# A hybrid attention and DeltaNet layer on one core: the inverse's solved blocks are loaded into the inverse's own buffer, and the delays of the work streams are set anew

## The chip, the core and the metric

One NeuronCore of a Trainium2 chip runs the whole layer as one program. It has a matrix engine (TensorE, PE in the rows, with its weight loads as PEld), a vector engine (VectorE, DVE), a scalar engine (ScalarE, ACT), GpSimd (POOL) and a queue engine (SyncE, SP) that issues DMA transfers; POOL issues some too. Every engine takes its own list of instructions strictly in order, and they wait for one another through semaphores. The metric is the device time of one execution in microseconds (us). Before the change the median of three runs was 639.21 us (635.7 to 640.05).

## The reference, cut to what matters

One sequence of 512 tokens, model width 1024, fp32. One input projection feeds eight heads of block-sparse attention and eight heads of gated DeltaNet; their outputs are joined, projected, normed and added to x, and a squared-ReLU MLP with 4096 hidden columns follows.

```python
h = rms_norm(x, pre_mix_norm[l])
proj = jnp.einsum('bsd,dc->bsc', h, w_in[l])
...
o_att = moba_attention(q, k, v, rel_bias)       # 8 heads of 64, blocks of 256 keys
...
# gated DeltaNet, chunks of 64 tokens, per head and chunk:
m = jnp.where(strict, jnp.einsum('bhnid,bhnjd->bhnij', k_beta, kc) * decay, 0.0)
a_mat = m + jnp.eye(C, dtype=jnp.float32)
uw = lax.linalg.triangular_solve(a_mat, rhs, left_side=True, lower=True, unit_diagonal=True)
u, w = uw[..., :dh], uw[..., dh:]
def step(state, xs):                             # over the 8 chunks
    v_new = u_c - jnp.einsum('bhck,bhkv->bhcv', w_c, state)
    o = jnp.einsum('bhck,bhkv->bhcv', q_c, state) + jnp.einsum('bhcs,bhsv->bhcv', a_c, v_new)
    state = state * gl[..., None, None] + jnp.einsum('bhck,bhcv->bhkv', k_c, v_new)
...
x = x + rms_norm(mix, post_mix_norm[l])
m = jnp.square(jax.nn.relu(rms_norm(x, ...) @ w_up)) @ w_down
x = x + rms_norm(m, post_mlp_norm[l])
```

## The kernel before

**Matmuls.** Each fp32 product is made of three matmuls of split operands (`mm3`: high by high, high by low, low by high). So every weight chunk is loaded to `w_raw` (two buffers), cast to `w_hi` on ACT (line 205), and its low part `w_lo` is taken by a subtraction on DVE or POOL (line 206). The string `LO` says for each chunk which of the two: 'v' for DVE, 'p' for POOL. Results stand in PSUM banks named ps_mm, ps_g and ps_a.

**Order of the work.** The kernel is written as some thirty generators ("streams"): `projections`, `chunks` (the DeltaNet operands), `inverse`, `scan`, `scores` and `values` (attention), `weights_out`, `output` and others. A small class `Weave` runs them against a virtual clock, `weave.now`, that advances by the columns of each matmul. A stream yields a delay (from the tables `WAIT` and `DELAY`) or the name of a mark that another stream sets, and is resumed when the clock has come that far; among those that are due the lower `RANK` goes first. PE's order is the order in which this loop emits matmuls, and is fixed by hand. DVE, ACT, POOL and, for most of the program, SP get their order from a scheduler with priorities (`LEAD`, `PRIO`). `ORDER` and `START` say in which order the projection's column groups come and when streams are started.

**The solve.** The triangular solve of each 64 by 64 chunk is done by halves of 32. `inverse()` inverts all diagonal 32 by 32 blocks at once on DVE, 31 steps of a product (line 880) and a subtraction (line 881) with partitions as blocks, makes the transposed blocks (line 884), and stores both to two DRAM tensors, `d_u` (line 885) and `d_t` (line 886). `scan()` loads them back in the layout that PE wants: `UT` (128 x 2048, a buffer of the shared tag `big`, which has 14 of them, zeroed by POOL on line 892) takes four loads of `d_u` (line 900), and two small tiles `uap` take four loads of `d_t` (line 897). Then three groups of matmuls follow: `p1` (128 of 32 by 32, `NT` by `uap`), copied back into `uap` by ACT (line 913); `p2` (128 of 32 by 32, `uap` by `UT`), whose negative goes into the missing corner of `UT` (line 926); and the products of `UT` with `kB` and `vB`. With these the scan over the chunks begins, in which the state `S` goes from PE to DVE (lines 999, 1000) and back.

**After the mix.** Each of four row tiles of 128 tokens is normed (lines 1124 to 1135: statistics on ACT, a power on POOL at line 243, the product `xs` on DVE at line 1135), then turned by eight transposes on PE, and feeds the MLP. POOL adds split operands for the MLP on line 1347.

Of the kernel before, what the change touches and what calls it, by code (L numbers as in the profile page):

```python
# [19 lines left out]
WAIT = {'h': 0.26, 'conv_k': 5.48, 'k': 6.88, 'conv_q': 8.11, 'q': 1.52, 'conv_v': 12.72, 'v': 2.29, 'z': 11.49, 'ab': 0.67, 'g': 9.16, 'scalars': 55.01, 'r_in': 0.0, 'r_out': 30.56, 'kk': 3.56, 'kk_out': 93.91, 'gl': 0.0, 'qk': 13.83, 'va': 1.36, 'a': 6.03, 'row': 1.56, 'rows': 4.29, 'pv': 2.34, 'att': 1.98, 'inverse': 0.76, 'merge': 6.6, 'p1': 2.26, 'p2': 223.99, 'w': 1.15, 'vn': 1.06, 'state': 0.64, 'o_in': 5.67, 'o': 1.23, 'wo': 1.48, 'wo_out': 0.86, 'normed3': 7.36, 'normed': 18.07, 'n': 2.53, 'up': 2.92, 'sums': 0.12, 'turned': 11.21, 'pv0': 3.36, 'wv': 3.58}  # L20

RANK = {'chunks': 5, 'inverse': 3, 'scan': 2, 'scores': 5, 'values': 4, 'finish_o': 2, 'take': 1}
LEAD = {'chunks': 30, 'inverse': 100, 'scan': 100, 'scores': 0, 'values': 0, 'finish_o': 100, 'take': 300, 'take_a': 100}
# [1612 lines left out]
```

## Time and profile before

| | before |
|---|---|
| median of three runs | 639.21 us (639.21, 635.7, 640.05) |
| the profiled execution's own time | 639.11 us |
| its span, first to last instruction | 637.3 us |
| mean granted TensorE clock | 0.993 of 2.4 GHz |
| busy share PE, DVE, ACT, POOL | 97%, 76%, 58%, 21% |

The span is 1.8 us shorter than the execution's own time, and that execution lies 0.1 us below the median. In a row of the timeline the first number is the start, the second the duration of the group (or the time from the first start to the last end), and in brackets at the end stands how long the engine was idle before and which instruction ended that. A matmul's duration includes its way through the array; matmuls in a row start 0.23 us apart at 512 columns, so starts, not durations, tell PE's pace. "PEclk" is the granted clock as a share of 2.4 GHz: 0.50 is 1.2 GHz.

### The profile page before, as it was taken

To read this page: it belongs to the slowest core of one execution; us is meant where nothing else is said; L and a number is where in the kernel's file an instruction comes from. 1 tells how busy PE (TensorE), PEld (TensorE's weight loads), DVE (VectorE), ACT (ScalarE), POOL (GpSimd) and SP (SyncE) were. 2 spreads that over 40 slices of the span, in tenths; PEclk is the share of its full clock that TensorE was granted. 3 is DMA by queue.
4 is the path that set the end of the run, shared out by engine and by line. 5 is a ranking of instruction groups with operands and counts; after the bars stand their busy time and mean duration, and the time that the engine had idled before them with its cause. 6 is when DMAs were issued, how large, how long until landed. Compare 5 with 4: busy or idle time off the path is not lost.

```text
span 637.3 us, 11091 instructions
## 1 busy us (share of the span) xinstructions
PE 620.8 (97%) x4291; PEld 535.8 (84%) x4291; DVE 484.4 (76%) x725; ACT 370.3 (58%) x620; POOL 136.1 (21%) x173
## 2 busy tenths in 40 slices
...
PEclk9999999999979999999999999999999999999999
...
GB/s 223 131 76 65 101 100 143 107 102 146 113 120 37 41 61 138 247 96 166 117 361 248 175 296 241 255 262 233 280 257 340 298 291 285 261 212 298 180 0 133
DMA packets 61270, 115.26 MB, mean 181 GB/s; under 512 B 15862, under 2 KB 35449, under 8 KB 60834
## 3 DMA queue, kind: packets, MB, share of 16 engines
...
q10 hardware_dynamic: 294, 0.27, 0.1%
q14 instruction: 18, 0.15, 0.1%
...
## 4 chain that ended last, share of the span: by engine, by line
PE 81%; DVE 6%; DMA 5%; ACT 3%; POOL 1%; issue 1%; SPq 1%; POOLq 0%; DVEq 0%; ACTq 0%
PE ps_mm L148 40%; PE ps_g L148 22%; PE ps_a L148 16%; DMA wo_raw<-in_w_out 1%; PE ps_a L152 1%; DMA xx<-in_x 1%; PE ps_g L152 1%; DVE conv L488 1%; DMA wd<-d_T 1%; DVE S L999 1%; DMA nb<-in_pre_mix 1%; DMA uap<-d_t 1%; DVE S L1000 1%; POOL oss L243 1%; SPq L900 1%
## 5 line engine op out<-in xcount | busy, mean ns | idle before, releaser
L181 ACT CAST wdh<-wd 128x1024 fp32r<-128x1024 f32 x53 | 55.6, 1050 | 51.2 <-PE ps_mm L148 23.6
L182 DVE TENSOR_TENSOR u_l<-w,u_h 128x1024 fp32r<-128x1024 f32 x46 | 56.2, 1224 | 37.9 <-ACT u_h L181 37.9
L182 DVE TENSOR_TENSOR wdl<-wd,wdh 128x1024 fp32r<-128x1024 f32 x53 | 64.9, 1225 | 22.8 <-ACT wdh L181 22.7
L181 ACT CAST u_h<-w 128x1024 fp32r<-128x1024 f32 x46 | 47.8, 1044 | 57.2 <-PE ps_a L148 19.8
L148 PE MATMUL ps_mm<-hT_h,w_hi 128*128 128x512 f32 (+1 forms) x192 | 76.4, 403 | 0.2 <-ACT hT_h L314 0.2
L148 PE MATMUL ps_mm<-hT_h,w_lo 128*128 128x512 f32 (+1 forms) x192 | 72.9, 385 | 0.0
L148 PE MATMUL ps_mm<-hT_l,w_hi 128*128 128x512 f32 (+1 forms) x192 | 72.6, 383 | 0.0
L1306 POOL DMA_DIRECT2D d_T<-in_w_down x32 | 33.1, 1034 | 143.6 <-DMA d_T<-in_w_down 82.3
L205 ACT CAST w_hi<-w_raw 128x512 fp32r<-128x512 f32 x56 | 34.8, 622 | 37.0 <-PE ps_mm L148 15.9
L206 POOL TENSOR_TENSOR w_lo<-w_raw,w_hi 128x512 fp32r<-128x512 f32 x21 | 27.2, 1294 | 97.2 <-ACT w_hi L205 94.2
L148 PE MATMUL ps_mm<-wdh,u_h 128*128 128x512 f32 x116 | 45.2, 390 | 0.0
L148 PE MATMUL ps_mm<-wdl,u_h 128*128 128x512 f32 x116 | 45.1, 389 | 0.0
L148 PE MATMUL ps_mm<-wdh,u_l 128*128 128x512 f32 x116 | 45.1, 389 | 0.0
L148 PEld LDWEIGHTS ps_mm<-hT_h,w_lo 128*128 128x128 f32 x192 | 35.8, 189 | 7.5
L148 PEld LDWEIGHTS ps_mm<-hT_h,w_hi 128*128 128x128 f32 x192 | 36.0, 190 | 6.6 <-issue 0.5
L148 PEld LDWEIGHTS ps_mm<-hT_l,w_hi 128*128 128x128 f32 x192 | 36.1, 190 | 5.4
L182 DVE TENSOR_TENSOR u_l<-f,u_h 128x1024 fp32r<-128x1024 f32 x28 | 34.1, 1218 | 0.0
L148 PE MATMUL ps_g<-wdh,u_h 128*128 128x512 f32 x80 | 31.2, 390 | 0.4 <-DVE y L1480 0.4
L148 PE MATMUL ps_g<-wdh,u_l 128*128 128x512 f32 x80 | 31.1, 389 | 0.0
L148 PE MATMUL ps_g<-wdl,u_h 128*128 128x512 f32 x80 | 31.1, 389 | 0.0
L206 DVE TENSOR_TENSOR w_lo<-w_raw,w_hi 128x512 fp32r<-128x512 f32 x35 | 24.4, 696 | 8.2 <-ACT w_hi L205 7.1
L488 DVE SCALAR_TENSOR_TENSOR conv<-ps_mm,cw,conv 128x511 f32<-128x511 f32 (+2 forms) x36 | 26.8, 746 | 4.1 <-ACT conv L485 3.4
(461 smaller groups left out, 1867.4 us busy)
## 6 DMA issues: line engine op xcount, KB each, us to landing
d_T<-in_w_down POOLq DMA_DIRECT2D x48, 512.0 KB, 10.8
wd<-d_T SPq DMA_DIRECT2D x32, 512.0 KB, 6.2
w<-in_w_up SPq DMA_DIRECT2D x28, 512.0 KB, 7.7
wd<-in_w_down SPq DMA_DIRECT2D x24, 512.0 KB, 6.7
w_raw<-in_w_in SPq DMA_DIRECT2D x46, 256.0 KB, 2.7
wo_raw<-in_w_out SPq DMA_DIRECT2D x16, 256.0 KB, 2.9
d_T<-d_T POOLq DMA_DIRECT2D x8, 512.0 KB, 11.0
xx<-in_x SPq DMA_DIRECT2D x4, 512.0 KB, 7.4
```

What stands on the lines that cost most here:

```text
L148: nc.tensor.matmul(o, l, r, **kw)
L152: nc.tensor.transpose(o, i, ident[:k, :k])
L181: nc.scalar.copy(hi, src)
L182: tt(lo, src, f32(hi), op=OP.subtract)
L205: nc.scalar.copy(hi, raw)
L206: (sub or tt)(lo, raw, f32(hi), op=OP.subtract)
L243: nc.gpsimd.tensor_tensor(r, r, m, op=OP.pow)
L488: stt(c[:, s:], p[:, :512 - s], cw[:, ft, j:j + 1], c[:, s:], op0=OP.mult, op1=OP.add)
L900: nc.sync.dma_start(z3(UT[32 * b:32 * b + 32, :, :, o:o + 32]), d_u[b].rearrange("z j i -> j z i"))
L999: tt(Sn[hs, :, hs], S[hs, :, hs], EGL[hs, :, n:n + 1].to_broadcast([64, 4, 64]), op=OP.mult)
L1000: tt(Sn[hs, :, hs], Sn[hs, :, hs], sp[n][cs, hh::2], op=OP.add)
L1306: nc.gpsimd.dma_start(d_T[t][k], block(b, second)[k], accum_op=OP.add, max_dma_last_dim=1024)
```

## The change

The solved blocks, which `inverse()` holds in one tile `inv` of 128 x 2048, are viewed there as `UT`. Right behind the two stores, six loads bring the blocks back in PE's layout into that same tile, and two POOL memsets of 32 x 32 x 32 clear the corners. `scan()` no longer has a `UT` buffer of its own, its memset or its eight loads; `p1` reads the transposed blocks from the corner of `UT` that `p2`'s result overwrites later. The tables are new: of `WAIT` 36 entries differ, of `DELAY` 123, of `PRIO` 38; five weight chunks more have their low part on DVE.

```diff
-RANK = {'chunks': 5, 'inverse': 3, 'scan': 2, 'scores': 5, 'values': 4, 'finish_o': 2, 'take': 1}
+RANK = {'chunks': 1, 'inverse': 1, 'scan': 1, 'scores': 5, 'values': 4, 'finish_o': 3, 'take': 1}
...
-LO = 'ppvvpvpvpppvvvvppvvvvvvvvvvvvvvvpvvppvvvppppvppvppvvvpvvvvvvvvvv'
+LO = 'ppvvpvpvvppvvvvpvvvpvvvvvvvvvvvvvvvvppvvvvvpvppvppvvvpvvpvvvvvvv'
...
     def inverse():
...
         nc.sync.dma_start(d_t.rearrange("b z j i -> (b z) (j i)"), iT.rearrange("p j i -> p (j i)"))
+        UT = inv.rearrange("p a j i -> p (a j i)").rearrange("p (h t e) -> p h t e", h=8, t=4)
+        merged.append(UT)
+        for c in range(2):
+            nc.sync.dma_start(z3(UT[left[c], :, :, second]), d_t[2 * c].rearrange("z j i -> j z i"))
+        for c in range(2):
+            nc.sync.dma_start(z3(UT[right[c], :, :, second]), d_u[2 * c + 1].rearrange("z j i -> j z i"))
+        for c in range(2):
+            nc.sync.dma_start(z3(UT[left[c], :, :, first]), d_u[2 * c].rearrange("z j i -> j z i"))
+            nc.gpsimd.memset(UT[right[c], :, :, first], 0.0)
         mark("inverse")
...
     def scan():
-        UT = big("UT", (128, 8, 4, 64))
-        nc.gpsimd.memset(UT, 0.0)
-        uap = [sc.tile([128, 4, 4, 32], FT, name="uap", tag="ot", bufs=4) for _ in range(2)]
-        z3 = lambda a: a.rearrange("p h t i -> p (h t) i")
-        for c in range(2):
-            for z in range(2):
-                nc.sync.dma_start(z3(uap[z][64 * c:64 * c + 32]), d_t[2 * c, 16 * z:16 * z + 16].rearrange("z j i -> j z i"))
-        for b in range(4):
-            o = 32 * (b % 2)
-            nc.sync.dma_start(z3(UT[32 * b:32 * b + 32, :, :, o:o + 32]), d_u[b].rearrange("z j i -> j z i"))
+        UT = merged[0]
+        half = [sc.tile([128, 4, 4, 32], FT, name="half", tag="ot", bufs=4) for _ in range(2)]
         yield WAIT["merge"]
...
-                        mm(p1[b, h, t], NT[a, 4 * z + h, t, 32:64], uap[z][a, h, t], start=True, stop=True,
+                        mm(p1[right[c], h, t], NT[left[c], 4 * z + h, t, second], UT[left[c], 4 * z + h, t, second], start=True, stop=True,
...
-                        mm(p2[a, h, t], uap[z][b, h, t], UT[b, 4 * z + h, t, 32:64], start=True, stop=True,
+                        mm(p2[left[c], h, t], half[z][right[c], h, t], UT[right[c], 4 * z + h, t, second], start=True, stop=True,
```

What moves, as the instruction lists of the two programs have it (line numbers of the change are two to six higher). First SP around the stores and the loads of the solved blocks; `w_raw` are weight chunks of the projection, `E`, `pt` and `wo_raw` belong to attention and the out projection. Before:

```order
L885 DMA d_u<-inv 128x1024
L200 DMA w_raw<-in_w_in 128x512
L886 DMA d_t<-inv 128x1024
L200 DMA w_raw<-in_w_in 128x512 x5
L784 DMA E<-d_e 128x512
L200 DMA w_raw<-in_w_in 128x512 x3
L784 DMA E<-d_e 128x512
L200 DMA w_raw<-in_w_in 128x512
L744 DMA pt<-pt 64x1024
L900 DMA UT<-d_u 32x32x32 x4
L744 DMA pt<-pt 64x1024
L897 DMA uap<-d_t 32x16x32 x4
```

With the change:

```order
L892 DMA d_u<-inv 128x1024
L893 DMA d_t<-inv 128x1024
L202 DMA w_raw<-in_w_in 128x512
L897 DMA inv<-d_t 32x32x32 x2
L899 DMA inv<-d_u 32x32x32 x2
L901 DMA inv<-d_u 32x32x32
L202 DMA w_raw<-in_w_in 128x512
L901 DMA inv<-d_u 32x32x32
L202 DMA w_raw<-in_w_in 128x512 x5
L786 DMA E<-d_e 128x512
L202 DMA w_raw<-in_w_in 128x512 x2
L786 DMA E<-d_e 128x512
```

The loads of the solved blocks have moved from behind ten weight chunks and a `pt` transfer to right behind the stores, ahead of the second and third weight chunk from there; two loads fewer are issued.

Second PE at the start of the program; `ident,xs` are the transposes of x's tiles, `w_150` is a column group of the input projection whose low part POOL makes. Before:

```order
L148 MATMUL ps_mm<-hT_h_83,w_150 128x256 x4
L148 MATMUL ps_mm<-hT_l_85,w_150 128x256 x4
L148 MATMUL ps_mm<-hT_h_83,w_150 128x256 x4
L152 MATMUL ps_g<-ident,xs_134 128x128 x8
L152 MATMUL ps_a<-ident,xs_134 128x128 x8
L148 MATMUL ps_a<-L,rb 8x512
```

With the change:

```order
L150 MATMUL ps_mm<-hT_h_83,w_150 128x256 x4
L154 MATMUL ps_g<-ident,xs_134 128x128 x8
L150 MATMUL ps_mm<-hT_l_85,w_150 128x256 x4
L150 MATMUL ps_mm<-hT_h_83,w_150 128x256 x4
L154 MATMUL ps_a<-ident,xs_134 128x128 x8
L150 MATMUL ps_a<-L,rb 8x512
```

The first eight transposes stand ahead of the last eight matmuls of this group, no longer behind them.

Third PE in the out projection, at the transposes of the third row tile (`ident,xs`; `wo_h,ma_h` and the like are the out projection, `ma_h,wu` the MLP's first products). Before:

```order
L148 MATMUL ps_mm<-mg_h,w_hi 128x256
L148 MATMUL ps_mm<-mg_l,w_hi 128x256
L148 MATMUL ps_mm<-mg_h,w_lo 128x256
L152 MATMUL ps_a<-ident,xs 128x128 x8
L148 MATMUL ps_mm<-ma_h,wu 128x256
L148 MATMUL ps_mm<-ma_l,wu 128x256
```

With the change:

```order
L150 MATMUL ps_g<-wo_h,ma_h 128x512
L150 MATMUL ps_g<-wo_l,ma_h 128x512
L150 MATMUL ps_g<-wo_h,ma_l 128x512
L154 MATMUL ps_a<-ident,xs 128x128 x8
L150 MATMUL ps_mm<-wo_h,ma_h 128x512
L150 MATMUL ps_mm<-wo_l,ma_h 128x512
L150 MATMUL ps_mm<-wo_h,ma_l 128x512
```

These transposes have moved ahead of the last six matmuls of the out projection and of 24 matmuls of the MLP.

## Rows read from the trace of the kernel before

**Rows 1.** The page: busy time of each engine (share of the span), and the granted TensorE clock in 40 slices of the span.

```profile
PE 620.8 (97%) x4291; PEld 535.8 (84%) x4291; DVE 484.4 (76%) x725; ACT 370.3 (58%) x620; POOL 136.1 (21%) x173
...
PEclk9999999999979999999999999999999999999999
```

**Rows 2.** Stretches of the span: from and to, length, then busy time of PE, PEld, DVE, ACT and POOL with their instructions, the granted clock, the DMA share and GB/s.

```profile
180.00:200.00 20.00, 18.36 (x366) 14.94 (x364) 8.12 (x17) 13.75 (x28) 5.40 (x6) 0.83 0.33 68
220.00:240.00 20.00, 18.00 (x270) 14.35 (x269) 14.93 (x28) 12.00 (x22) 4.84 (x8) 1.00 0.24 68
```

**Rows 3.** The view of waits, PE's: what PE waited for: the waiting matmul, what it waited for, us in total, times, the longest.

```profile
PE ps_g L148 <- DVE S L1000: 2.8, 3, 1.4
PE ps_g L148 <- DMA uap<-d_t: 1.6, 2, 0.9
...
PE ps_a L152 <- DVE mins L798: 0.5, 1, 0.5
```

**Rows 4.** PE's timeline through p1 (`uap,NT`) and p2 (`UT,uap`).

```profile
183.13 0.24 PE L148 MATMUL ps_g<-uap,NT 32*32 32x32 f32 x2 [0.91 <-DMA uap<-d_t]
184.11 3.53 PE L148 MATMUL ps_g<-uap,NT 32*32 32x32 f32 x126 [0.74 <-DMA uap<-d_t]
187.57 0.80 PE L148 MATMUL ps_mm<-hT_h,w_hi 128*128 128x512 f32 x1
...
191.13 0.40 PE L148 MATMUL ps_mm<-hT_l,w_hi 128*128 128x512 f32 x1
191.36 0.40 PE L148 MATMUL ps_mm<-hT_h,w_lo 128*128 128x512 f32 x1
191.69 2.21 PE L148 MATMUL ps_g<-UT,uap 32*32 32x32 f32 x128
193.83 0.61 PE L148 MATMUL ps_a<-kt,pt 128*128 128x384 f32 x2
```

**Rows 5.** Two short stretches of the same kind as rows 2, one in p1 and one in p2.

```profile
186.00:188.00 2.00, 2.00 (x61) 1.94 (x58) 0.21 (x1) 1.93 (x4) 0.00 (x0) 0.50 0.04 10
...
192.00:194.00 2.00, 2.00 (x122) 1.96 (x116) 1.68 (x3) 1.49 (x4) 0.00 (x0) 1.00 0.04 8
```

**Rows 6.** SP's timeline: when it issued the store of the transposed blocks and the eight loads.

```profile
145.23 0.33 SPq L886 DMA_DIRECT2D d_t<-inv  x1
...
174.66 3.35 SPq L900 DMA_DIRECT2D UT<-d_u  x4
...
179.02 2.74 SPq L897 DMA_DIRECT2D uap<-d_t  x4
```

**Rows 7.** DMA issues from 140 to 190 us: what was moved, count, KB each, median us from issue to landing.

```profile
w_raw<-in_w_in SPq DMA_DIRECT2D x12, 256.0 KB, 2.9
...
d_t<-inv SPq DMA_DIRECT2D x1, 512.0 KB, 4.2
```

**Rows 8.** The instructions on the tile `UT`, here its four loads: least, median and longest duration on the queue in ns, first and last start; and their landing.

```profile
L900 SPq DMA_DIRECT2D UT<-d_u x4: 577/770/1098, 174.7 to 177.3; - x4
...
DMA to landing us min/median/max: 4.1/4.2/4.7
```

**Rows 9.** Timeline of ACT, DVE and PE around the weight chunk that comes second behind `d_t`'s store on SP: its cast (153.61), its low part (154.79) and the matmul that first reads it (160.47); and, at 154.37, the first matmul that reads the low part of the chunk two before it.

```profile
153.61 0.62 ACT L205 CAST w_hi<-w_raw 128x512 fp32r<-128x512 f32 x1 [1.55 <-DMA w_raw<-in_w_in]
154.37 0.39 PE L148 MATMUL ps_mm<-hT_h,w_lo 128*128 128x512 f32 x1
154.79 0.68 DVE L206 TENSOR_TENSOR w_lo<-w_raw,w_hi 128x512 fp32r<-128x512 f32 x1
...
160.47 0.39 PE L148 MATMUL ps_mm<-hT_h,w_hi 128*128 128x512 f32 x1
```

**Rows 10.** Timeline of POOL: the making of a chunk's low part, and the memset of the old `UT` buffer.

```profile
168.63 1.29 POOL L206 TENSOR_TENSOR w_lo<-w_raw,w_hi 128x512 fp32r<-128x512 f32 x1 [3.21 <-ACT w_hi L205]
170.27 1.81 POOL L892 MEMSET UT<- 128x2048 f32 x1 [0.36 <-PE ps_a L148]
```

**Rows 11.** Timeline of PE and ACT at the start of the program.

```profile
17.22 0.74 PE L148 MATMUL ps_mm<-hT_h,w 128*128 128x256 f32 x4 [0.44 <-POOL w L206]
17.80 1.03 PE L152 MATMUL ps_g<-ident,xs 128*128 128x128 f32 x8
18.34 0.30 ACT L181 CAST abw<-abr 128x128 fp32r<-128x128 f32 x1 [2.73 <-POOL picks L461]
...
21.10 0.38 PE L148 MATMUL ps_a<-L,rb 33*8 33x128 f32 x2 [0.44 <-DVE hT_l L182]
```

**Rows 12.** Timeline of DVE and PE: the last product within the chunks (`LWQ,kraw`), and the DVE instruction that makes its operand.

```profile
94.16 0.69 DVE L693 TENSOR_TENSOR kraw<-kraw,ps_g 128x512 f32<-128x512 f32 x1
...
95.92 0.32 PE L148 MATMUL ps_g<-LWQ,kraw 64*64 64x128 f32 x1
```

**Rows 13.** Timeline of DVE, POOL and PE at the norms of the row tiles.

```profile
293.84 1.28 DVE L1135 SCALAR_TENSOR_TENSOR xs<-xs,s,nb 128x1024 f32<-128x1024 f32 x1 [0.94 <-POOL s L243]
...
304.74 2.39 POOL L1347 TENSOR_TENSOR g<-ma_h,ma_l 128x1024 f32<-128x1024 f32 x1
304.74 3.48 DVE L1135 SCALAR_TENSOR_TENSOR xs<-xs,s,nb 128x1024 f32<-128x1024 f32 x1
...
311.40 1.04 PE L152 MATMUL ps_a<-ident,xs 128*128 128x128 f32 x8
313.06 0.38 PE L148 MATMUL ps_mm<-ma_h,wu 128*128 128x256 f32 x1 [0.63 <-DVE xs L1129]
```

More of the change, by code (lines that the diff above doesn't have):

```diff
@@ L18 @@
 EPS = 1e-6
-WAIT = {'h': 0.26, 'conv_k': 5.48, 'k': 6.88, 'conv_q': 8.11, 'q': 1.52, 'conv_v': 12.72, 'v': 2.29, 'z': 11.49, 'ab': 0.67, 'g': 9.16, 'scalars': 55.01, 'r_in': 0.0, 'r_out': 30.56, 'kk': 3.56, 'kk_out': 93.91, 'gl': 0.0, 'qk': 13.83, 'va': 1.36, 'a': 6.03, 'row': 1.56, 'rows': 4.29, 'pv': 2.34, 'att': 1.98, 'inverse': 0.76, 'merge': 6.6, 'p1': 2.26, 'p2': 223.99, 'w': 1.15, 'vn': 1.06, 'state': 0.64, 'o_in': 5.67, 'o': 1.23, 'wo': 1.48, 'wo_out': 0.86, 'normed3': 7.36, 'normed': 18.07, 'n': 2.53, 'up': 2.92, 'sums': 0.12, 'turned': 11.21, 'pv0': 3.36, 'wv': 3.58}
-RANK = {'chunks': 5, 'inverse': 3, 'scan': 2, 'scores': 5, 'values': 4, 'finish_o': 2, 'take': 1}
-LEAD = {'chunks': 30, 'inverse': 100, 'scan': 100, 'scores': 0, 'values': 0, 'finish_o': 100, 'take': 300, 'take_a': 100}
+WAIT = {'h': 0.17, 'conv_k': 5.51, 'k': 6.88, 'conv_q': 8.11, 'q': 1.44, 'conv_v': 12.31, 'v': 1.09, 'z': 11.49, 'ab': 1.31, 'g': 9.16, 'scalars': 15.81, 'r_in': 2.78, 'r_out': 105.83, 'kk': 3.56, 'kk_out': 79.98, 'gl': 0.4, 'qk': 12.04, 'va': 2.7, 'a': 10.02, 'row': 1.54, 'rows': 4.29, 'pv': 2.86, 'att': 0.47, 'inverse': 1.05, 'merge': 7.68, 'p1': 2.18, 'p2': 2268.35, 'w': 0.0, 'vn': 0.84, 'state': 0.27, 'o_in': 13.03, 'o': 0.31, 'wo': 2.02, 'wo_out': 1.48, 'normed3': 6.75, 'normed': 14.59, 'n': 4.75, 'up': 5.18, 'sums': 0.0, 'turned': 11.67, 'pv0': 3.41, 'wv': 2.81}
+RANK = {'chunks': 1, 'inverse': 1, 'scan': 1, 'scores': 5, 'values': 4, 'finish_o': 3, 'take': 1}
+LEAD = {'chunks': 100, 'inverse': 300, 'scan': 300, 'scores': 30, 'values': 30, 'finish_o': 30, 'take': 300, 'take_a': 30}
 FILL = (8, 3, 0)
@@ L28 @@
 VBANKS = ('mm', 'mm', 'a', 'a')
-START = (1.86, 1.69, 7.77, 14.48, 18.11, 17.11, 68.08)
-ORDER = 'k0 k1 q0 q1 q2 k2 q3 k3 x0 y0 z0 w x1 v2 v0 y1 v1 v3 x2 y2 z2 x3 z1 y3 z3'
-DELAY = {"projections.84": 0.19, "turned3": 1.48, "inverse": 1.14, "inverse.14": 3.11, "projections.173": 0.0, "values.15": 5.25, "scan.3": 0.96,
[58 rows of a table removed]
-PRIO = {'weights_out.16': 20, 'projections.11': 0, 'chunks3.7': 60, 'output.56': 60, 'projections.54': 20, 'output.58': 20, 'output.59': 0, 'projections.75': 60, 'projections.71': 20, 'scores.19': 400, 'output.50': 400, 'projections.117': 0, 'projections.3': 0, 'projections.70': 150, 'inverse.26': 150, 'output.46': 150, 'output.24': 400, 'projections.16': 60, 'scores.6': 400, 'inverse.17': 60, 'x3.1': 400, 'output.11': 150, 'values.40': 150, 'projections.13': 0, 'projections.9': 60, 'scores.9': 400, 'scan.2': 60, 'inverse.9': 60, 'output.68': 150, 'projections.93': 60, 'scores.34': 400, 'weights_out.12': 150, 'w0.1': 400, 'output.51': 150, 'scores.15': 0, 'inverse.25': 150, 'scan.15': 0, 'output.53': 20, 'projections.196': 20, 'projections.83': 60, 'chunks1.3': 20, 'values.18': 400, 'v0.1': 150, 'projections.34': 0, 'output.66': 150, 'scan.18': 400, 'chunks2.4': 150, 'chunks2.5': 20, 'projections.31': 400, 'scores.39': 0, 'y2.1': 20, 'z3.1': 60, 'output.19': 60}
@@ L93 @@
-LO = 'ppvvpvpvpppvvvvppvvvvvvvvvvvvvvvpvvppvvvppppvppvppvvvpvvvvvvvvvv'
+START = (5.11, 1.21, 12.77, 13.69, 16.56, 17.9, 66.19)
+ORDER = 'k0 k1 q0 q1 q2 k2 q3 k3 x0 y0 z0 w v2 x1 v0 y1 v1 v3 x2 y2 z2 x3 z1 y3 z3'
+DELAY = {"projections.84": 0.69, "turned3": 1.48, "inverse": 1.14, "inverse.14": 3.11, "projections.173": 0.0, "values.15": 5.25, "scan.3": 0.96,
[60 rows of a table added]
+PRIO = {'weights_out.16': 20, 'projections.11': 0, 'chunks3.7': 60, 'output.56': 60, 'output.58': 20, 'output.59': 0, 'projections.75': 60, 'projections.71': 20, 'scores.19': 400, 'output.50': 400, 'projections.117': 0, 'projections.3': 0, 'projections.70': 150, 'inverse.26': 150, 'output.46': 150, 'projections.16': 60, 'scores.6': 400, 'inverse.17': 60, 'x3.1': 400, 'output.11': 150, 'values.40': 150, 'projections.13': 0, 'projections.9': 60, 'scores.9': 400, 'scan.2': 60, 'inverse.9': 60, 'output.68': 150, 'projections.93': 60, 'scores.34': 400, 'weights_out.12': 150, 'w0.1': 400, 'inverse.25': 150, 'scan.15': 0, 'output.53': 20, 'projections.196': 20, 'projections.83': 60, 'chunks1.3': 20, 'v0.1': 150, 'projections.34': 0, 'output.66': 150, 'scan.18': 400, 'chunks2.4': 150, 'chunks2.5': 20, 'projections.31': 60, 'scores.39': 0, 'z3.1': 60, 'weights_out.10': 60, 'weights_out.6': 400, 'projections.195': 400, 'projections.88': 20, 'projections.112': 150, 'projections.84': 150, 'weights_up.9': 0, 'scores.17': 0, 'projections.125': 60, 'projections.10': 150, 'chunks1.5': 150, 'inverse.23': 20, 'chunks3.3': 400, 'projections.140': 20, 'projections.67': 150, 'chunks3.4': 150, 'projections.43': 20, 'projections.177': 20, 'w1.1': 400, 'scan.21': 20, 'finish_o3.1': 60, 'projections.78': 20, 'projections.132': 400, 'projections.23': 20, 'k2.1': 150, 'inverse.24': 20, 'projections.200': 0, 'q2.2': 150, 'scan.5': 20, 'output.31': 400}
@@ L866, in values @@
             mark(f"att{p}", WAIT["att"])
+    merged = []
+    left, right = ([slice(64 * c + o, 64 * c + o + 32) for c in range(2)] for o in (0, 32))
+    first, second = slice(0, 32), slice(32, 64)
+    z3 = lambda a: a.rearrange("p h t i -> p (h t) i")
     def inverse():
@@ L886, in inverse @@
         nc.sync.dma_start(d_t.rearrange("b z j i -> (b z) (j i)"), iT.rearrange("p j i -> p (j i)"))
+        UT = inv.rearrange("p a j i -> p (a j i)").rearrange("p (h t e) -> p h t e", h=8, t=4)
[7 more added lines that the diff above has]
+            nc.gpsimd.memset(UT[right[c], :, :, first], 0.0)
         mark("inverse")
     def scan():
[L891 to L900 removed]
+        UT = merged[0]
+        half = [sc.tile([128, 4, 4, 32], FT, name="half", tag="ot", bufs=4) for _ in range(2)]
         yield WAIT["merge"]
         for z in range(2):
+            zs = slice(4 * z, 4 * z + 4)
             p1 = bank(shape=(128, 4, 4, 32))
@@ L907, in scan @@
                     for c in range(2):
-                        a, b = slice(64 * c, 64 * c + 32), slice(64 * c + 32, 64 * c + 64)
-                        mm(p1[b, h, t], NT[a, 4 * z + h, t, 32:64], uap[z][a, h, t], start=True, stop=True,
+                        mm(p1[right[c], h, t], NT[left[c], 4 * z + h, t, second], UT[left[c], 4 * z + h, t, second], start=True, stop=True,
                            tile_position=(64 * c, 64 * c + 32))
             for c in range(2):
-                b = slice(64 * c + 32, 64 * c + 64)
-                nc.scalar.copy(uap[z][b], p1[b])
+                nc.scalar.copy(half[z][right[c]], p1[right[c]])
         mark("p1")
@@ L916, in scan @@
         for z in range(2):
+            zs = slice(4 * z, 4 * z + 4)
             p2 = bank(shape=(128, 4, 4, 32))
```

3 lines of the change are left out of this document (1 added, 2 removed), and 118 rows, old and new, of the table DELAY.

## The prediction

> **What bounds the kernel now.** I began with the page. PE is busy for 97% of the span, no other engine for more than 76% [rows 1]: PE's own work sets the time, and a change of order can only win what PE loses to waits and to its clock. The clock line has one slice below 9 in the middle, at about 180 us [rows 1], and the stretch 180 to 200 shows both losses: PE idle for 1.64 of 20 us, and a granted clock of 0.83 [rows 2]. The view of waits names the cause: 1.6 us in two waits for the loads of `uap`; the largest entry, three waits of 2.8 us for the scan's state `S`, lies elsewhere [rows 3]. PE's timeline shows the place: 0.91 and 0.74 us idle ahead of p1's first and third matmul [rows 4], and then p1 at a clock of 0.50, 1.2 GHz, while p2, as many matmuls of the same size, runs at 1.00 [rows 5].
>
> Why the loads were late is in SP's timeline. The transposed blocks were stored at 145.23, but the loads were issued at 174.66 and 179.02 [rows 6], after the memset of a `UT` buffer that came free only at 170.27 [rows 10]. The data lay ready for more than 25 us.
>
> **The change, part by part.** I make the sum against the profiled execution's own 639.11 us, 0.1 below the median of the runs.
>
> *The wait at p1* (removed). d_t's store was issued at 145.23. DVE now makes five more low parts (0.68 each [rows 9]), one of which may stand ahead of the last steps of the inverse, so I put the store at 145.9. It lands 4.2 us later [rows 7], at 150.1. Six loads at 3.35 / 4 = 0.84 us of queue each [rows 6] and a weight chunk between them are issued by 155.5 and, by the slowest landing of the old ones, 4.7 us [rows 8], are there at 160.2. PE reaches p1 at about 181: more than 20 us to spare. The two memsets stand behind the same stores and clear half as many columns as the old one, which took 1.81 us [rows 10]: 0.9 each, done by 152. Gain 0.91 + 0.74 = 1.65 us [rows 4]. Next late would be what p1 and p2 read besides, and that was ready long before.
>
> *The clock* (a consequence). From 184.11 to 187.57 p1's 126 matmuls took 3.46 us; p2's 128 took 2.14 (191.69 to 193.83), or 2.11 for 126: 1.35 us lost. From 187.57 to 191.13 eight matmuls of 512 columns took 3.56 us; at the 0.23 between the starts at 191.13 and 191.36 they take 1.84: 1.72 lost [rows 4]. Together 3.07. The other bound is the clock itself: 0.83 over 20 us is (1 - 0.83) x 2 x 20 = 6.8 us at half rate [rows 2], worth at most 3.4. I take 3.1, since it is measured on the work itself.
>
> That the clock stays up without the wait is the step I am least sure of. Rows for it: p2's small matmuls at 1.00 [rows 5], and the stretch 220 to 240, in which PE was idle for 2.0 of 20 us in shorter pieces, at 1.00 throughout [rows 2]. The Trainium skill speaks against it (page "TensorE: Matmul & The Clock Gate", section "A second HAM failure mode: psum-queue depth-cycling"): there a kernel whose matmuls came in groups with brief idles between them had its clock swing between the two levels, with no long wait. By that rule the groups of tiny matmuls in p1 could lower the clock with their data in time, and the sum would be 637.3; by the rows it is 634.2.
>
> *Weight chunks behind the loads on SP* (a queue passed). SP takes its list in order, so the second chunk behind d_t's store now stands behind five loads, which wait for the stores. Its issue comes at 150.1 + 5 x 0.84 = 154.3; landing 2.9 later [rows 7], cast 0.62, low part 0.68 [rows 9]: ready at 158.5. PE first reads it at 160.47 [rows 9], about 159.8 with the gain at the start below. Cost nothing, with 1.3 us of cover. On POOL the first memset stands ahead of a low part of 1.29 us [rows 10]: 150.1 + 0.9 + 1.3 = 152.3, read by PE at 154.37 [rows 9], or 153.7; 1.4 us of cover there. Between 174 and 184 SP loses eight issues and POOL 1.81 us; neither is waited for there by anything but p1, so nothing is gained beside it.
>
> *The start.* PE waits 0.44 us at 17.22 for a low part from POOL [rows 11]. Eight transposes (1.03 us) now stand ahead of that point, ready by then, and cover it: 0.44 gained. The second wait, 0.44 at 21.10 for `hT_l` [rows 11], hangs on ACT, which sat idle for 2.73 us until 18.34 behind an instruction that waits for POOL [rows 11]; with the transposes earlier it may go too. Between nothing and 0.44 I take half: 0.65 gained in all.
>
> *The last product within the chunks* comes six matmuls earlier, 6 x 0.23 = 1.4 us: from 95.92 to 94.5, while its operand is ready at 94.16 + 0.69 = 94.85 [rows 12]. Cost 0.3. Other products and transposes move by one to six us against the projection between 80 and 172 us; PE had no idle time there, so nothing can be gained, and I keep a cost of 0 to 1 us for the range.
>
> *The third tile's transposes* pass six matmuls of 0.23 and 24 of half that, 4.25 us: from 311.40 to 307.15. Their `xs` was ready at 304.74 + 3.48 = 308.22: the usual 1.28 was stretched beside a POOL addition of 2.39 that began at the same moment [rows 13]. Both come right behind the same POOL result in the new lists too, so I let it be stretched again: PE waits 1.1 us. The 0.63 at 313.06 [rows 13] is then gone, because PE comes there later. Net cost 0.45; were `xs` not stretched, 0.
>
> *The end of attention.* The wait for `mins`, 0.5 us [rows 3], lies where a score product and its DVE step are now earlier. Between nothing and 0.5 I take 0.25 gained.
>
> *The scan* has the same order on PE, ACT and DVE as before, and the MLP too, with PE fully busy. Nothing there.
>
> Sum: -1.65 - 3.1 - 0.65 + 0.3 + 0.45 - 0.25 = -4.9, so 634.2 us. With the ends of these terms (clock 3.4, start 0.9, attention 0.5, no cost) it is 632.7; with the clock at 2.6, no gain at the start or in attention, the two costs and 1 us of small waits, it is 636.6. Of a measurement of this kernel 1% (6.4 us) is about what can be told from no change; my forecast lies just inside.
>
> **The rivals.**
>
> *The clock falls all the same.* Then only the idle time goes: 634.2 + 3.1 = 637.3. For it: the fall came within p1 itself, and p1's matmuls are as small as before. Against it: rows 2 and 5 as above.
>
> *The scan takes the gain back.* PE waits three times for `S` [rows 3], which goes round between PE and DVE. If something with a time of its own sets that pace (a weight load, a cast), PE arrives 4.75 us earlier and waits 4.75 us longer: 634.2 + 4.75 = 638.95. Against it: those loads start when PE and ACT free a buffer, and so move with PE.
>
> *The scan's waits shrink too.* DMA and POOL are less crowded ahead of the scan; if what stands before `S` on DVE comes earlier, up to 2.8 us [rows 3] go: 631.4. Against it: the lists there are unchanged.
>
> *Slower: the stores hold up SP's queue.* Place: the second weight chunk behind d_t's store. It decides from the point at which that chunk lands after 158.5 (159.8 less 0.62 and 0.68). By the upper rows, 1.1 us of queue for each load and a landing of 4.7 [rows 8], it is 150.1 + 5.5 + 4.7 = 160.3: PE idles 1.8 us. Such an idle time was followed at p1 by 3.1 us lost to the clock [rows 4, 5]. ACT, which takes its list in order, would hold the attention's exponentials behind the late cast for 6.7 us (160.3 against 153.61 [rows 9]), for which I estimate 1.5 us more. 634.2 + 1.8 + 3.1 + 1.5 = 640.6, slower than before. For it: the new loads have runs of the same size as the old ones of `UT`, one of which needed 1.1 us of queue. Against it: a weight chunk landed in 2.9 us in this very stretch [rows 7].
>
> That the loads are not early after all, because a wait holds them, I leave out: the list has them right behind the stores, and they need nothing but these.
>
> **How the numbers follow.** The forecast has a chance of 0.50, the clock 0.15, the scan taking it back 0.10, the scan's waits shrinking 0.15, the held queue 0.10. The range 630.5 to 640.0 leaves out the better part of the fourth case and the worse half of the last, and what nobody thought of: some 15%. The forecast's own range is 632.7 to 636.6. Faster by over 1% means below 632.8: most of the fourth case and a third of the first (its better end and the spread of the runs), 0.30. Slower by over 1% means above 645.6, beyond every case; I leave 0.06 for several of the costs at once. Within 1%: 0.64.
>
> **What would show it.** Right: no wait for a load in PE's list at p1, a clock of 1.00 between 175 and 195, p1 in about 2.1 us, 19.9 of 20 us busy there; a wait of about 1 us at the third tile's transposes and 0.3 at the last product within the chunks. Wrong: a clock below 0.9 at p1 (first rival), waits for `S` of more than 5 us (second), or PE waiting for ACT's cast or a low part at 158 to 165 us (last).

## The result and the profile after

The changed kernel takes 633.77 us (median of 9 runs, 632.38 to 634.90) against 639.31 for the kernel before (9 runs, 635.48 to 640.05): a ratio of 0.9921, 95% interval 0.9900 to 0.9943. The forecast was 634.2. The profiled execution took 634.15 us, with a span of 632.4: 4.9 us less than before, as much as the sum had said. The parts of that sum did not all come out, though. Of the 38 executions of the kernel before that were taken beside the experiments, one took 3272.45 us and is left out of all that follows.

The page of the changed kernel, busy time and granted clock [rows 1]:

```profile
PE 618.2 (98%) x4291; PEld 532.9 (84%) x4291; DVE 481.6 (76%) x730; ACT 369.9 (58%) x620; POOL 130.3 (21%) x169
...
PEclk9999999999999999999999999999999999999998
```

The two stretches of rows 2 (length, busy time of PE, PEld, DVE, ACT, POOL, then clock, DMA share, GB/s):

```profile
180.00:200.00 20.00, 20.00 (x456) 16.57 (x454) 9.55 (x23) 17.14 (x37) 9.60 (x9) 1.00 0.13 42
220.00:240.00 20.00, 18.08 (x234) 14.19 (x234) 13.93 (x24) 11.20 (x20) 6.10 (x9) 1.00 0.23 70
```

PE's waits [rows 3]: no load is among them any more.

```profile
PE ps_g L150 <- DVE S L1006: 2.7, 3, 1.4
...
PE ps_a L154 <- DVE mins L800: 0.5, 1, 0.5
PE ps_mm L150 <- DVE conv L490: 0.5, 1, 0.5
```

PE's timeline through p1 (`inv,NT`) and p2 (`inv,half`) [rows 4]:

```profile
182.46 2.21 PE L150 MATMUL ps_g<-inv,NT 32*32 32x32 f32 x128
184.61 0.50 PE L150 MATMUL ps_mm<-hT_h,w_hi 128*128 128x512 f32 x1
...
187.12 2.21 PE L150 MATMUL ps_g<-inv,half 32*32 32x32 f32 x128
189.26 0.62 PE L150 MATMUL ps_a<-kt,pt 128*128 128x384 f32 x2
```

p1 has no wait and takes 2.15 us from its first start to the next product, as p2 does. From p1's first matmul to the product behind p2 it is 6.80 us; before it was 10.70 from 183.13 and 0.91 of waiting ahead of it, 11.61 together [rows 4]. That gives 4.81 us, nearly the whole result. The rest, by comparing the start of each matmul in both traces: 0.88 gained by 37.98 (now 37.10), 1.1 lost in small waits from there to p1, 0.1 lost at the end of attention, 0.65 gained at the third row tile, and 0.2 lost behind the MLP.

### The profile page after: what moved, and what is told of

It reads as the page before. It is cut to its first block, busy times and chain, and to the rows that moved or that the text cites. A ratio compares the mean times of both kernels' runs of the same rounds, so it can differ in the third digit from the quotient of the medians.

```text
span 632.4 us, 11086 instructions
## 1 busy us (share of the span) xinstructions
PE 618.2 (98%) x4291; PEld 532.9 (84%) x4291; DVE 481.6 (76%) x730; ACT 369.9 (58%) x620; POOL 130.3 (21%) x169
## 4 chain that ended last, share of the span: by engine, by line
PE 82%; DVE 8%; ACT 4%; DMA 3%; issue 1%; POOL 1%; SPq 0%; POOLq 0%; DVEq 0%; ACTq 0%
PE ps_mm L150 39%; PE ps_g L150 24%; PE ps_a L150 16%; PE ps_a L154 2%; DMA wo_raw<-in_w_out 2%; DVE conv L490 1%; PE ps_g L154 1%; DMA w_raw<-in_w_in 1%; DVE w_lo L208 1%; DMA d_t<-inv 1%; DVE S L1005 1%; DVE pt L745 1%; DVE pl L184 1%; DVE S L1006 1%; POOL oss L245 1%
## 5 line engine op out<-in xcount | busy, mean ns | idle before, releaser
L208 POOL TENSOR_TENSOR w_lo<-w_raw,w_hi 128x512 fp32r<-128x512 f32 x16 | 20.6, 1288 | 93.8 <-PE ps_a L150 56.0
L208 DVE TENSOR_TENSOR w_lo<-w_raw,w_hi 128x512 fp32r<-128x512 f32 x40 | 27.5, 688 | 12.0 <-ACT w_hi L207 10.9
L183 ACT CAST u_h<-f 128x1024 fp32r<-128x1024 f32 x28 | 29.3, 1046 | 0.0
```

What stands on the lines that cost most here:

```text
L183: nc.scalar.copy(hi, src)
L208: (sub or tt)(lo, raw, f32(hi), op=OP.subtract)
```

## The experiments

### Each half of the change by itself

The new code with the old tables (1a), and the new tables with the old `UT`, `uap` and their loads (1b). 1a in short, with every table as before:

```diff
+        UT = inv.rearrange("p a j i -> p (a j i)").rearrange("p (h t e) -> p h t e", h=8, t=4)
...
+            nc.sync.dma_start(z3(UT[left[c], :, :, second]), d_t[2 * c].rearrange("z j i -> j z i"))
```

> The kernel before with the new loads and the tiles they need, and all tables as before, so that PE, DVE and ACT have the same order as before. If the gain comes from the early loads: no wait for a load at p1, a clock of 1.00 from 180 to 200, every matmul after p2 about 4.8 us earlier than before and the waits at the start (0.44, 0.44), at 254 us and at 313 us (0.63) as they were; 639.3 - 4.8 = 634.5 us, ratio 0.9925. If p1's tiny matmuls lower the clock by themselves: only 1.65 us, about 637.7. If the new tables carry the gain: 639.3.

> The changed kernel's tables with the old loads, their old place, the old UT buffer and its memset. If the loads carry the gain: two waits for uap at p1 of 1.5 to 2 us together and half the clock for some 7 us; 0.9 us won at the start, 1.1 lost again from 40 to 180 us, 0.65 won at the norms: 639.3 - 0.4 = 638.9 us. If the tables carry it: about 634.5.

1a: 636.65 us (635.57 to 639.0, 10 runs), ratio 0.9972 (0.9952 to 0.9992). 1b: 638.71 (637.31 to 640.56, 10 runs), ratio 1.0009 (0.9989 to 1.0028). So the tables alone are worth nothing that can be measured, and the new loads alone some 1.8 us, not the 4.8 of p1. The trace of 1a has p1 without a wait, at full clock, with the same 4.81 us gained there; but 1.64 us are lost at 164 to 166: ahead of that PE is 0.19 us behind the kernel before, after it 1.83. Its timeline of SP, ACT, DVE and PE:

```profile
149.64 1.12 SPq L895 DMA_DIRECT2D inv<-d_t  x2
...
152.07 1.55 SPq L899 DMA_DIRECT2D inv<-d_u  x2
153.67 9.46 SPq L200 DMA_DIRECT2D w_raw<-in_w_in  x4
...
157.89 0.62 ACT L205 CAST w_hi<-w_raw 128x512 fp32r<-128x512 f32 x1 [3.62 <-PE ps_a L148]
160.01 0.73 ACT L800 ACTIVATE L<-L,mins 128x512 f32<-128x512 f32 x1 [1.49 <-DVE mins L798]
...
158.55 0.69 DVE L206 TENSOR_TENSOR w_lo<-w_raw,w_hi 128x512 fp32r<-128x512 f32 x1 [2.75 <-ACT w_hi L205]
159.27 0.69 DVE L798 CUSTOM_DVE_ANT_0 L<-ps_a,E 128x512 f32<-128x512 f32 x1
...
166.98 0.52 PE L152 MATMUL ps_a<-ident,L 128*128 128x128 f32 x3 [0.80 <-DVE mins L798]
```

SP stood until 149.64 for the store, issued six loads, and only then the next weight chunk, at 153.67. ACT sat idle for 3.62 us ahead of that chunk's cast. (The engine named in the bracket is PE, but PE had long released its bank; what came last was the chunk.) DVE stood until 158.55 for that cast, to make the chunk's low part, and only then came to the attention's step that adds the bias to the scores and takes the minimum (`mins`), at 159.27. In the kernel before it had begun at 156.23:

```profile
156.23 0.69 DVE L798 CUSTOM_DVE_ANT_0 L<-ps_a,E 128x512 f32<-128x512 f32 x1
```

The exponential on ACT needs `mins`: ACT was idle for 1.49 us more behind the cast, until 160.01, and PE waited for what follows. This is the slower rival's place, with a smaller price. Its mechanism is nearly the same, but the list that holds the exponential up is DVE's; ACT's own was past the cast at 158.5. In the changed kernel SP does nearly the same:

```profile
148.78 0.93 SPq L897 DMA_DIRECT2D inv<-d_t  x2
149.75 1.29 SPq L899 DMA_DIRECT2D inv<-d_u  x2
151.09 0.81 SPq L901 DMA_DIRECT2D inv<-d_u  x1
151.94 0.71 SPq L202 DMA_DIRECT2D w_raw<-in_w_in  x1
...
157.20 0.62 ACT L207 CAST w_hi<-w_raw 128x512 fp32r<-128x512 f32 x1 [3.54 <-DMA w_raw<-in_w_in]
157.85 0.69 DVE L208 TENSOR_TENSOR w_lo<-w_raw,w_hi 128x512 fp32r<-128x512 f32 x1 [2.69 <-ACT w_hi L207]
158.57 0.62 ACT L207 CAST w_hi<-w_raw 128x512 fp32r<-128x512 f32 x1 [0.75 <-DMA w_raw<-in_w_in]
159.21 0.69 ACT L487 ACTIVATE conv<-ps_mm,cw 128x512 f32<-128x512 f32 x1
...
162.88 0.47 PE L150 MATMUL ps_mm<-hT_h,w_hi 128*128 128x512 f32 x1 [0.45 <-DVE conv L490]
```

ACT is idle for 3.54 us again. But behind the late cast the new tables have another cast and a convolution, not the exponential; on DVE the score's step comes at 160.60 behind two low parts and a convolution step, and PE waits for none of it but the convolution, 0.45 us. How much is left is not fixed: in six other profiles with the new tables and the loads on SP, whose edits lie behind this place, the same wait is 0.91 (3a below), 0.36 (3b) and four times none.

### The same loads, from another queue

To show that SP's queue is the cause, the six loads are issued by POOL, once with the old tables (2a) and once in the changed kernel (2b). All else stays as it is in 1a and in the changed kernel.

```diff
-            nc.sync.dma_start(z3(UT[left[c], :, :, second]), d_t[2 * c].rearrange("z j i -> j z i"))
+            nc.gpsimd.dma_start(z3(UT[left[c], :, :, second]), d_t[2 * c].rearrange("z j i -> j z i"))
```

> This is the kernel with the tables of before and the new loads, with the six loads issued from POOL's queue instead of SP's. Theory (SP's queue): the 1.83 us that the new loads lost between 164 and 168 came from the weight chunk that stood behind the six loads on SP, issued at 153.67. With the loads off SP that chunk is issued at about 149.6, its cast is done before 155, the two waits on the mins in front of the transposes fall back to under 0.5 us, and the median goes from 636.65 to 634.8, with p1 still without a wait and the clock at 1.00. Rival 1 (the old tables are short there for other reasons, the scores' rows moved by the inverse's end): the waits on the mins stay at 1.6, and the time stays at 636.6. Rival 2 (POOL's queue holds up low parts that POOL makes, 1.3 us each, behind the loads): the waits on the mins go, a wait on w_lo of 1 us or more comes in the stretch from 150 to 165, and the time is 636 or more.

> This is the changed kernel with the six loads issued from POOL's queue instead of SP's. Theory (SP's queue is covered by the new tables but for some 0.45 us): the weight chunks between 149 and 154 are issued some 3 us earlier, which takes away at most the 0.45 us that PE waited at 162.88 in the changed kernel's profile, so the time is 633.3 to 633.8, the same within the measurement. Rival (POOL's low parts wait behind the loads): a wait on w_lo of 1 us or more between 150 and 170, and 634.8 or more. Second rival (the changed tables were fitted to SP's order, and weight chunks that run ahead take buffers or bandwidth): new waits elsewhere before 180, 634.5 or more.

2a: 634.23 us (633.53 to 635.46, 5 runs), ratio 0.9938 (0.9919 to 0.9957). 2b: 633.49 (632.77 to 634.9, 4 runs), ratio 0.9921 (0.9897 to 0.9945). From 2a's timeline, POOL, SP and ACT:

```profile
148.58 1.88 POOL L895 DMA_DIRECT2D inv<-d_t  x2 [3.45 <-DVE mx L864]
...
145.15 14.32 SPq L200 DMA_DIRECT2D w_raw<-in_w_in  x5
...
153.06 0.62 ACT L205 CAST w_hi<-w_raw 128x512 fp32r<-128x512 f32 x1 [2.25 <-DMA w_raw<-in_w_in]
...
155.90 0.73 ACT L800 ACTIVATE L<-L,mins 128x512 f32<-128x512 f32 x1 [1.61 <-DVE mins L798]
```

SP goes on with its weight chunks, the cast comes 4.8 us and the exponential 4.1 us earlier than in 1a, and the waits at 164 to 166 are gone. Some 1.4 us of both is a lead that 2a's profile has over 1a's from the start and from 124 us, ahead of the loads; behind the place of the waits the lead is 3.07, so the queue is worth 1.64 in the traces, as 1a had lost. With the old tables the medians differ by 2.4 us. The two kernels ran on different chips; by their ratios to the kernel before beside each it is 0.0034, 2.2 us, with 0.002 of uncertainty on either ratio, which does not tell 2.2 from 1.64. Under the new tables it is worth nothing that can be measured. So most of what the new tables add to the new loads is cover for SP's held queue, and an edit of three lines that takes the loads off SP does it too. POOL's low parts did not suffer: in 2a PE waits 0.4 us for one at the longest, as before.

### Does idle time lower the clock?

In the forecast the clock's recovery was the least certain step. Four kernels put an idle time of TensorE in front of p1 in the changed kernel, through a DVE step on a bank, whose result, zero, is added to a column of `UT`. The first two have 13 matmuls of 512 columns besides, whose result is not used: all of them ahead of the idle time (3a), or 1 ahead and 12 between it and p1 (3b). 3a:

```diff
...
+        for i in range(13):
+            mm(gap, ident_r, masks, start=True, stop=True, skip_group_check=True)
+        for i in range(2):
+            nc.vector.tensor_scalar(zero[:, :512], (zero if i else gap)[:, :512], 0.0, None, op0=OP.mult)
+        for c in range(2):
+            tt(UT[left[c], 0, 0, 32:33], UT[left[c], 0, 0, 32:33], zero[left[c], 0:1], op=OP.add)
```

> The changed kernel with 13 matmuls of 512 columns in front of p1 whose result isn't needed, and then an idle time of TensorE of about 1.5 us (a round trip over DVE, whose result, zero, is added to one column of UT) right before p1. The 13 matmuls cost 2.8 us at the full clock, the idle time 1.5. Theory (idle time directly ahead of p1's and p2's small matmuls lets the granted clock fall): the granted clock is 0.50 for 3 to 7 us somewhere between p1's start and 12 us later, and the time is 639.5 to 641.5. Rival (the fall in the kernel before had to do with the DMA wait itself or with a longer stretch of light work): the clock stays at 1.00, and the time is 633.8 + 2.8 + 1.5 = 638.1.

> The same work as in the run before, in another order: 1 of the 13 matmuls, the idle time of about 1.5 us, 12 matmuls of 512 columns (2.6 us of full work), and then p1. Theory (what counts is the idle time together with the small matmuls behind it): the clock stays at 1.00 through p1 and p2, and the time is 638.1. Rival (the idle time alone lets the clock fall, whatever follows): the granted clock is 0.50 for 3 us or more within 10 us of the idle time, and the time is 639.5 or more. If neither this run nor the run before shows a fall, the idle time of 1.5 us is not enough by itself.

Neither lowered the clock: 639.66 and 639.28 us, a clock of 1.00 in every stretch from 184 to 205. Taken alone that speaks for the rival, that an idle time is not enough. 3b's PE timeline:

```profile
184.66 0.43 PE L150 MATMUL ps_g<-inv,NT 32*32 32x32 f32 x4 [2.14 <-DVE inv L919]
185.01 3.03 PE L150 MATMUL ps_g<-picks 128*128 128x512 f32 x12
187.97 2.21 PE L150 MATMUL ps_g<-inv,NT 32*32 32x32 f32 x128
```

But both have 2.8 us of full work next to the idle time. So two more runs with only 1 of the 13, with the idle time in one piece (3c) and, as in the kernel before, in two (3d; there a second DVE step and addition hold up the fifth and later of p1's 128 matmuls):

> The changed kernel with one matmul of 512 columns and then an idle time of TensorE of about 2.1 us in one piece directly ahead of p1, and nothing between that idle time and p1 (the two runs with 13 extra matmuls around an idle time of 1.43 and 2.14 us showed a clock of 1.00 throughout). Theory (idle time of this length lets the clock fall when the work around it is p1's small matmuls, as in the kernel before): a stretch at 0.50 of 3 to 7 us between 183 and 195, and 637.6 to 639.5. Rival (no idle time of 2 us is enough by itself, the fall in the kernel before needs something more): the clock stays at 1.00, and the time is 633.8 + 0.2 + 2.1 = 636.1.

> The same with the idle time in two pieces, as in the kernel before: some 1.3 us, two of p1's small matmuls, some 0.7 us, and then the rest of p1. Theory (idle in two pieces around two small matmuls, as it was before, lets the clock fall): a stretch at 0.50 of 3 to 7 us between 183 and 195, and 637.6 to 639.5. Rival (idle time of this size is not enough by itself): the clock stays at 1.00 and the time is 636.1. If the clock falls here and not in the run with one piece, what counts is the order of light work and idle time; if it falls in both, the full work around the idle time was what kept the clock up in the runs with 13 matmuls.

The clock fell in both. 3c's PE timeline, and its stretches:

```profile
183.97 2.77 PE L150 MATMUL ps_g<-inv,NT 32*32 32x32 f32 x128 [2.14 <-DVE inv L918]
186.66 0.80 PE L150 MATMUL ps_mm<-hT_h,w_hi 128*128 128x512 f32 x1
...
190.29 2.21 PE L150 MATMUL ps_g<-inv,half 32*32 32x32 f32 x128
192.43 0.62 PE L150 MATMUL ps_a<-kt,pt 128*128 128x384 f32 x2
```

```profile
184.00:186.00 2.00, 2.00 (x110) 1.95 (x112) 0.78 (x2) 0.60 (x2) 0.00 (x0) 0.92 0.33 116
186.00:188.00 2.00, 2.00 (x30) 1.74 (x26) 0.00 (x0) 1.71 (x3) 0.00 (x0) 0.50 0.02 4
188.00:190.00 2.00, 2.00 (x8) 1.49 (x7) 0.18 (x1) 0.77 (x2) 0.00 (x0) 0.73 0.00 0
190.00:192.00 2.00, 2.00 (x110) 1.72 (x110) 1.97 (x5) 1.15 (x3) 0.00 (x0) 1.00 0.03 8
```

After the idle time p1 begins at 1.00 and drops to 0.50 before it ends; p2 is back at 1.00. From the start of p1's main run of matmuls to the product behind p2, the same work everywhere (within four of p1's 128 matmuls), each kernel takes:

```
kernel          idle ahead, us    p1 to behind p2, us    clock falls
before          0.91 + 0.74       9.72                   yes
1b              1.16 + 0.59       8.33                   yes
3c (one piece)  2.14              8.46                   yes
3d (two pieces) 1.41 + 0.26       8.47                   yes
3a (13 ahead)   1.43              6.99                   no
3b (12 behind)  2.14              6.81                   no
the change      none              6.80                   no
```

So an idle time of 1.65 to 2.14 us, with p1's small matmuls behind it, brought the clock down each time, whether a DMA or a DVE step caused it, and in one piece or two. The same 2.14 us with 4 small and then 12 full matmuls behind it did not (3b against 3c). 3a, with 13 ahead, did not either, but its idle time is also the shortest, so it alone would leave open which of the two mattered. Small matmuls without idle time did not lower it. The fall cost 1.5 to 1.7 us in three profiles and 2.9 in the one of before: how long it lasts differs from run to run. Each of these kernels ran once, so 3b against 3c is one pair. The totals, 640.02 us for 3c and 637.26 for 3d, lie on either side of the 637.6 to 639.5 that were expected; they also hold other differences, such as the one below.

The runs' own mean clocks fit this. Of 37 runs of the kernel before that stood beside the experiments, the five with a mean clock of 0.987 took 640.26 to 640.96 us, the four with 0.997 took 635.99 to 636.75. A line through all 37 has 0.38 us for each 0.001. The nine runs of the changed kernel have 0.995 to 0.998. At a clock of 0.997 the change is thus worth about 2.7 us (636.5, the mean of the four, against 633.8). As an estimate, the clock is worth 2.3 by the median of the 37 (638.75), and 2.8 by that of the nine runs above (639.3); it takes the four as runs without a fall at p1, which no trace shows. The wait at p1 is not all that lowers a mean clock, either: of the 16 runs of 2b and of the two kernels in the section on the scan's wait, none of which has a wait at p1 in its profile, four have a clock of 0.991 to 0.993 and take 634.35 to 636.12 us.

### The third row tile

In the changed kernel the third tile's transposes had no wait, where 1.1 us was forecast. Timeline of DVE, POOL and PE [rows 13]:

```profile
299.64 0.69 DVE L184 TENSOR_TENSOR ma_l<-ps_a,ma_h 128x512 fp32r<-128x512 f32 x1
300.25 1.29 DVE L1141 SCALAR_TENSOR_TENSOR xs<-xs,s,nb 128x1024 f32<-128x1024 f32 x1
...
299.67 0.55 POOL L245 TENSOR_TENSOR s<-s,mhalf 128x1 f32<-128x1 f32 x1
300.41 3.38 POOL L1353 TENSOR_TENSOR g<-ma_h,ma_l 128x1024 f32<-128x1024 f32 x1 [0.20 <-DVE ma_l L184]
...
302.69 1.03 PE L154 MATMUL ps_a<-ident,xs 128*128 128x128 f32 x8
```

Before, `xs` and POOL's addition `g` began together and `xs` took 3.48, `g` 2.39 [rows 13]. Now `g` still waits 0.20 us for `ma_l`, `xs` begins 0.16 earlier, takes 1.29, and `g` takes 3.38. One of the two is made to wait for the other. This agrees with the Trainium skill (page "SBUF — State Buffer", section "🔬 SBUF: two separate sides"): DVE and GpSimd share one pair of ports to SBUF as a lock, which the instruction that starts first keeps to its end. As a test, one small copy in front of `xs`:

```diff
+        if t == 2:
+            nc.vector.tensor_copy(sq[:, 0:256], x1[:, 0:256])
```

> The changed kernel with one small DVE copy (128x256, about 0.3 us) put ahead of the third tile's xs; what it writes is overwritten by xs. If DVE's product and POOL's addition exclude each other and the later one waits for the other's end: xs now starts after POOL's addition, takes about 3.4 us instead of 1.29, POOL's takes 2.4 instead of 3.38, PE waits about 1 us at the third tile's transposes, and every matmul of the MLP is 0.8 to 1.1 us later than in the changed kernel. If they only share bandwidth, or the stretch had another cause: xs stays at 1.3 to 1.6 us and is ready before PE comes, the MLP is not later by more than 0.1 us.

One run, 635.18 us. Against the matmuls ahead, the copy moves `s` and `xs` back by 0.21 us and `g` by 0.01. From its timeline:

```profile
300.15 2.40 POOL L1355 TENSOR_TENSOR g<-ma_h,ma_l 128x1024 f32<-128x1024 f32 x1
...
300.19 3.44 DVE L1143 SCALAR_TENSOR_TENSOR xs<-xs,s,nb 128x1024 f32<-128x1024 f32 x1
...
303.78 1.06 PE L154 MATMUL ps_a<-ident,xs 128*128 128x128 f32 x8 [1.20 <-DVE xs L1143]
```

With `xs` 0.04 us behind `g` the roles turn, PE waits 1.20 us, and all that follows comes about 1.3 us later against the changed kernel than what stands ahead of it. In the profiles of all kernels with the old tables (before, 1a, 2a) both start together and `xs` takes 3.47 or 3.48. With the new tables `xs` is ahead by 0.15 to 0.17 in every profile but two: this one, and 3c, where both started at 305.01, `xs` took 3.48 and PE waited 1.20.

### The scan's largest wait

Three waits for `S` make 2.7 us, the longest 1.4. DVE makes the low part of the first chunk of output weights right ahead of that step, at 234.54, and stood 1.96 us for the chunk's cast; given to POOL:

```diff
-                    load_split(wh[:, k], wl[:, k], w_out[512 * z + 128 * k:512 * z + 128 * k + 128, 512 * b:512 * b + 512],
+                    load_split(wh[:, k], wl[:, k], w_out[512 * z + 128 * k:512 * z + 128 * k + 128, 512 * b:512 * b + 512], (b, z, k) == (0, 1, 0) and nc.gpsimd.tensor_tensor,
```

> The changed kernel with the low part of the first out-projection chunk on POOL, so that DVE no longer holds the state's update S behind a low part that waits for the chunk's load. If that in-order wait makes the 1.40 us wait for S at 236 us: it goes, the matmuls after it are 1.1 to 1.4 us earlier than in the changed kernel, 632.5 us. If the state's round trip itself sets it: the wait stays above 1 us and the time at 633.8. If ACT's cast of the same chunk, which waits for the same load, takes its place: 0.2 to 0.6 us won.

633.16 us (632.79 to 634.72, 6 runs), ratio 0.9916 (0.9890 to 0.9943): the changed kernel's time. PE's waits show why:

```profile
PE ps_g L150 <- DVE S L1006: 1.4, 2, 0.8
...
PE ps_a L150 <- DVE kt L754: 1.0, 1, 1.0
PE ps_a L150 <- ACT wo_h L195: 0.5, 1, 0.5
```

The 1.4 is gone and PE gains 1.57 us at 236; a wait of 1.0 for `kt` and 0.5 for `wo_h` then take it back by 248. Here the second rival, the one in which the scan sets its own pace, has a grain of truth: behind `S` stands work that does not move with PE. The next two chunks of output weights land at 237.68 and 239.78 us, and at 237.87 and 239.76 in the changed kernel.

With the loads on POOL as well:

> The changed kernel with the two edits that each took a wait away: the six loads issued from POOL's queue (633.49 alone), and the low part of the second output weight's first chunk made by POOL (633.16 alone). If what each takes away stays away, 632.9 or less; theory: the gain of the second edit is given back at once, as when it ran alone, and the first gains at most 0.45 us, so the time is the changed kernel's within the measurement, 633.0 to 633.8. Rival (POOL becomes late with both): a wait on a POOL instruction of 1 us or more and 634.5 or more.

633.59 us (632.65 to 636.12, 6 runs), ratio 0.9919 (0.9894 to 0.9945). Neither edit nor both together beat the change by an amount that can be measured.

## Why the prediction was right

*The wait at p1 and the clock.* Both steps held: 4.81 us in the traces against 1.65 and 3.1 forecast. The memsets were done at 152.18 (152 forecast) and the loads landed in 5.3 us at most, long before p1. The reason given for the clock was only half of it: p2's full clock spoke against the small matmuls alone, rightly, and the idle time of 220 to 240 against idle time alone; the runs show that the two together did it. The value of 3.1 is that of a profile with a long fall; the estimate from the runs' clocks is 2.3 to 2.8, and three other profiles have 1.5 to 1.7. The rival in which the clock falls all the same did not come. The Trainium skill's rule behind it (page "TensorE: Matmul & The Clock Gate", section "A second HAM failure mode: psum-queue depth-cycling") speaks of brief idles between groups of matmuls. Here p1 without an idle time ahead stayed at 1.00, and with one of 1.65 us or more directly ahead it did not, so the traces agree with the rule but not with its use on p1 without the wait.

*Weight chunks behind the loads on SP.* This step had its end right by luck, and its price wrong. Forecast: low part ready at 158.5; measured: 157.85 + 0.69 = 158.54. But the chunk was issued at 151.94, not 154.3, since the store came 1.6 us earlier and five loads took 3.2 us of queue, not 4.2; and it landed 5.2 us after issue, not 2.9. The two errors cancel. The cost was set at nothing because PE reads the chunk later, and it does. What was overlooked in the sum is that ACT and DVE take their lists in order too, so that what stands behind the late cast and the late low part is late as well. The slower rival named this for ACT; in 1a it was DVE that held up the exponential. With the old tables that costs 1.64 us (1a, 2a), a third of the gain at p1. The new tables have other work there, and 0.45 us was left of it in the profile of the change, nothing to 0.91 in the others. The forecast came out because of a cover that it had not counted.

*The start.* 0.88 gained by 37.98, 0.65 forecast: both waits went, as its upper end had it. Profiles of one kernel's start differ by as much (1a and 2a, the same up to the loads, by 0.9 at 11 us), so the size is not certain.

*The last product within the chunks.* 0.3 forecast, nothing measured: it came at 93.61 without a wait. The forecast moved the product forward and held its operand at 94.85; the operand came 1.40 us earlier too, at 92.76 + 0.69 = 93.45.

*Small waits from 38 to 180.* About 1.1 us lost, the cost that was kept for the range alone: 0.45 at 162.88, 0.23 for `pl` at 175.52, the rest in smaller ones. The first of these stands in the window in which the prediction looked for the last rival; it is a wait for a convolution step, not for a cast or a low part.

*The third tile.* The sign was wrong: 0.65 gained, 0.45 lost forecast. The failed step is "both come right behind the same POOL result in the new lists too": `g` also needs `ma_l`, which now comes behind that result, so that `g` starts 0.16 us behind `xs`.

*The end of attention.* 0.25 gained forecast, 0.1 lost: the wait for `mins` stayed at 0.5. *The scan and the MLP* moved as one, as forecast.

Measured gain less forecast gain, in us: p1 and clock +0.06, start +0.23, chunks +0.3, third tile +1.1, small waits -1.1, attention -0.35, tail -0.2. The total hits because these cancel; with the gains alone it would have been 632.5, with the losses alone 635.9. That the profile's total, 634.15, is right to 0.1 us is luck; that p1 and the clock carry it is not.
